# The first load of x: one transfer of 128 partitions, or two of 64 from two queues

## The chip, the cores and the metric

The kernel runs on one core of one Trainium2 chip. Times are device microseconds of one execution. The profile is that of one execution, taken by the hardware profiler; its times count from the first instruction of the program on the chip.

## The reference

`x` has shape 16 x 512 x 768 in float32, which is 8192 tokens of 768 numbers. `A` is 768 x 16 and `B` is 16 x 768. The result is x plus a low-rank correction of it:

```
def reference(x, A, B, scale):
    lora = np.matmul(np.matmul(x, A), B)
    return (x + scale * lora).astype(np.float32)
```

With scale 0.5. x is 25.2 MB and is read once, the result is 25.2 MB and is written once; A and B are small.

## The kernel before, in words

The 8192 tokens stand as 64 tiles of 128 partitions by 768 numbers. They are cut into five parts of 8, 8, 16, 16 and 16 tiles (`PARTS`). Within a part a partition holds consecutive tokens, so that a load of n tiles reads one stretch of n x 3 KB from memory for each partition. All of x lives in one SBUF tensor, `x_sb`, with room for 48 tiles; the last 16 tiles take the places of the first 16 once these are stored.

**Loads and stores.** All transfers are issued from SyncE's queue (SP), in a fixed order. There are eight loads of x (`LOADS`, L106): load 0 has the first 2 tiles (768 KB, 6 KB for each partition), load 1 the other 6 tiles of the first part (2304 KB), loads 2, 3 and 4 have 8 tiles each, load 5 has 16, and loads 6 and 7 have 8 each. The sum is written back into `x_sb`, and five stores (`STORES`) take whole parts out to memory. `on_sync` (L135) issues load 0, load 1, then three small transfers with A (L155) after a wait for a memset of `a_rows`, one with B (L159), then loads 2 to 5 (L160). Then it waits for sums and for TensorE's progress, issues stores 0 and 1 (L170), issues load 6 when store 0 has landed and load 7 when store 1 has, and issues the last three stores as their sums are ready. Each load has a semaphore of its own, which a transfer raises by 16 when it has landed.

**The work on a group.** The tiles are worked on in groups of eight. ScalarE (ACT) narrows the first four tiles of a group to float16 and GpSimd (POOL) the other four (`narrowed`, L186, L194). VectorE (DVE) transposes the group in 32 x 32 blocks (L250). TensorE (PE) multiplies by A, spread out in `w_bd` (L281), ScalarE scales the small product into `y_bd` (L238), TensorE multiplies by B (L302), and VectorE adds the result to x in place (L255), two tiles at a time.

**The first group** is narrowed in smaller pieces: GpSimd takes the two tiles of load 0 (L209), ScalarE the two after them and then the last four (L228, L229), all of load 1. GpSimd then waits for B (L211) and lays out the weights. `narrowed` waits for the semaphore of each load that its tiles come from, once for each engine and load (L188 to L191).

ScalarE's stream starts with `narrowed` for tiles 2 and 3; ahead of that the compiler puts the load of its function table.

Of the kernel before, what the change touches and what calls it, by code (L numbers as in the profile page):

```python
# [28 lines left out]
def kernel(  # L29
# [10 lines left out]
    P = 128  # L40
# [3 lines left out]
    x2 = x.flatten_outer_dims()  # L44
# [38 lines left out]
    def sem(name):  # L83
        sems.append(nc.alloc_semaphore(name))
        return sems[-1]
# [10 lines left out]
    def memory(t2, i, s, n):  # L96
        S = PARTS[i]
        return t2[ds(parts[i], S * P), :].rearrange("(p s) d -> p s d", s=S)[:, ds(s, n), :]

    def held(i, s, n):  # L100
        return tiles(where.index((i, s)), n)

    def tiles(t, n):
        return x_all[:, ds(t % ROOM, n), :]

    LOADS = [  # L106
        (0, 0, 2), (0, 2, 6), (1, 0, 8), (2, 0, 8), (2, 8, 8), (3, 0, 16), (4, 0, 8), (4, 8, 8)
    ]
    s_load = [sem(f"s_load{k}") for k in range(len(LOADS))]

    def load_of(t):
        i, s = where[t]
        return next(k for k, ld in enumerate(LOADS) if ld[0] == i and ld[1] <= s < ld[1] + ld[2])
# [18 lines left out]
    section = ExitStack()  # L132
    section.enter_context(tc.tile_critical(no_gpsimd_drain=True))  # L133

    def on_sync(e):  # L135
        def load(k):
            ld = LOADS[k]
            e.dma_start(out=held(*ld), in_=memory(x2, *ld)).then_inc(s_load[k], 16)  # L138

        def summed(k):  # L140
            e.wait_ge(s_sum, k + 1)
            if STORED[k] + 1 < NG:

                e.sem_inc(s_free[PAIRS - 1], 1)

        def store(k, done):
            st = STORES[k]
            e.dma_start(out=memory(out2, *st), in_=held(*st)).then_inc(done, 16)

        load(0)  # L150
        load(1)
        e.wait_ge(s_ready, 1)
        blocks = A.rearrange("(c e) r -> c (e r)", e=64)
        for c in range(SETS):
            e.dma_start(  # L155
                out=a_rows[c : SET * SET : SET, :], in_=blocks[ds(c * SET, SET), :]
            ).then_inc(s_a, 16)
        e.wait_ge(s_brows, 1)
        e.dma_start(out=b_rows[0 : R * APART : APART, :], in_=B).then_inc(s_b, 16)  # L159
        for k in range(2, len(LOADS) - 2):  # L160
            load(k)

        for p in range(2, PAIRS):
            e.sem_inc(s_free[p], 1)
        summed(0)
        summed(1)


        e.wait_ge(s_lora, 2 * PAIRS + 2)
        store(0, s_out0)  # L170
        store(1, s_out1)
        e.wait_ge(s_out0, 16)
        load(len(LOADS) - 2)
        e.wait_ge(s_out1, 16)
        load(len(LOADS) - 1)
        for k in range(2, len(STORES)):
            summed(k)
            if k == 2:


                e.wait_ge(s_raise, 6)
            store(k, s_out)
# [3 lines left out]
    def narrowed(e, copy, g, first, n=SUB):  # L186
        t = g * GROUP + first
        for k in dict.fromkeys(load_of(t + k) for k in range(n)):  # L188
            if (e, k) not in here:
                here.add((e, k))  # L190
                e.wait_ge(s_load[k], 16)  # L191
        if g:
            e.wait_ge(s_taken, g)
        ins = copy(out=xn[:, ds(first, n), :], in_=tiles(t, n))  # L194

        ins.then_inc(s_narrow if g else s_first if first else s_a, 1)

    def on_gpsimd(e):
        e.memset(a_rows[0:Q], 0.0).then_inc(s_ready, 1)  # L199
        e.memset(b_rows, 0.0).then_inc(s_brows, 1)  # L200
        e.memset(pick, 0.0).then_inc(s_pick, 1)
        e.memset(w_bd.rearrange("p c k m -> p (c k m)").bitcast(fp32), 0.0)  # L202
        e.memset(y_bd.rearrange("p s m -> p (s m)").bitcast(fp32), 0.0).then_inc(s_ready, 1)  # L203
        e.wait_ge(s_pick, 1)
        e.affine_select(  # L205
            out=pick, in_=pick, compare_op=mybir.AluOpType.not_equal, fill=1.0, base=0,
            pattern=[[0, NQ], [-APART, Q]], channel_multiplier=1,
        ).then_inc(s_pick, 1)
        narrowed(e, e.tensor_copy, 0, 0, SUB // 2)  # L209
        e.wait_ge(s_pick, 2)  # L210
        e.wait_ge(s_b, 16)  # L211
        e.tensor_copy(out=b_half, in_=b_rows).then_inc(s_bh, 1)  # L212
        e.wait_ge(s_ready, 3)
        e.tensor_copy(  # L214
            out=w_one.rearrange("i (c e) k r -> i c e (k r)", c=SETS),
            in_=a_t[0:Q].rearrange("i k r (e c) -> i c e (k r)", c=SET)[:, 0:SETS, 0:SET, :],
        ).then_inc(s_w, 1)
        e.wait_ge(s_w, 1)
        for b in range(NQ):
            e.tensor_copy(  # L220
                out=w_bd[ds(b * Q, Q), :, :, ds(b * Q, R)], in_=w_one
            ).then_inc(s_w, 1)
            e.wait_ge(s_w, b + 2)
        for g in range(1, NG):
            narrowed(e, e.tensor_copy, g, SUB)

    def on_scalar(e):
        narrowed(e, e.copy, 0, SUB // 2, SUB // 2)  # L228
        narrowed(e, e.copy, 0, SUB)  # L229
        e.wait_ge(s_bp, 1)  # L230
        e.copy(out=b_mm, in_=lora[0][:, 0, :]).then_inc(s_bm, 1)  # L231
        for g in range(NG):
            if g + 1 < NG:
                narrowed(e, e.copy, g + 1, 0)
            e.wait_ge(s_y, g + 1)
            for b in range(NQ):
                q = ds(b * Q, Q)
                last = e.mul(out=y_bd[q, :, q], in_=y_ps[q, :, :], mul=sc)  # L238
            last.then_inc(s_spread, 1)
# [33 lines left out]
    def on_tensor(e):  # L273
# [58 lines left out]
        for p in range(PAIRS):  # L332
            raised(p)

    on_sync(nc.sync)
    on_gpsimd(nc.gpsimd)
    on_scalar(nc.scalar)
    on_vector(nc.vector)
    on_tensor(nc.tensor)
# [44 lines left out]
```

## Time and profile before

| | |
|---|---|
| median of 3 runs | 123.55 us (123.45 to 123.71) |
| profiled execution, span | 121.9 us (the one time that the page gives of it) |
| bytes moved | 50.43 MB, 414 GB/s over the span |
| DMA packets' share of 16 engines' span | 96.8% |
| VectorE, the busiest compute engine | 81.7 us, 67% |
| load 0: issued from, to landing | 0.97 us, 4.5 us later |
| load 1: landing, as seen by ScalarE | 11.1 us |
| stores: last issued | 101.0 us, 20.0 us to landing |

The profile's groups are named by line, engine and operation; L138 is the line that issues loads of x, L148 the one that issues stores. A transfer's row on SP's queue (SPq) is the time in which the queue was issuing it; the transfer itself runs later, on 16 DMA engines. In the answers by window, the DMA column is the mean busy share of these 16 engines and the last column the rate of the bytes; a packet is counted in the window in which it starts, which is why a share can stand a little above 1.

### The profile page before, as it was taken

The numbers are of one execution on the slowest core, as the hardware profiler recorded it, in microseconds if no ns is written. First come the engines' busy times: TensorE is split into PE (matmuls) and PEld (weight loads), VectorE is DVE, ScalarE is ACT, GpSimd is POOL, SyncE is SP. The second block draws the span as 40 slices with busy tenths as digits, with TensorE's granted clock in tenths as the row PEclk, the third lists the DMA queues.
The fourth block names the chain that finished last, engine by engine and source line by source line (L and its number), as shares of the span: only waits on it lengthen the run. The fifth ranks groups of instructions, "written<-read, shape, count | busy, mean of one in ns | idle before, by whom it ended". The sixth has DMA issues, their size and how long they took to land.

```text
span 121.9 us, 885 instructions
## 1 busy us (share of the span) xinstructions
PE 50.5 (41%) x322; PEld 29.3 (24%) x322; DVE 81.7 (67%) x42; ACT 37.4 (31%) x43; POOL 28.4 (23%) x24
## 2 busy tenths in 40 slices
PE   0000239487457457647756714774674320000000
PEld 0000026244233233424424402442442110000000
DVE  0003850799999999999999959999995991000000
ACT  4003929444426402917230093643004000000000
POOL 7732638044026002607100090630000000000000
PEclk9999999999999999999999999999999985555555
DMA  3999999999997996999989999998998999899890
GB/s 67 421 429 429 443 443 403 451 435 419 476 516 339 435 516 298 460 403 443 443 363 460 427 427 468 451 484 387 419 500 387 403 516 403 371 516 419 355 516 0
DMA packets 1928, 50.43 MB, mean 414 GB/s; under 512 B 236, under 2 KB 236, under 8 KB 392
## 3 DMA queue, kind: packets, MB, share of 16 engines
q1 hardware_dynamic: 1928, 50.43, 96.8%
HBM read 25.26 MB, written 25.17 MB: 414 GB/s over the span
## 4 chain that ended last, share of the span: by engine, by line
DVE 33%; DMA 29%; PE 9%; ACT 6%; POOL 2%; issue 2%; SPq 0%; DVEq 0%
DVE x_sb L255 21%; DMA x_sb<-in_x_dram 20%; DVE xt L250 12%; DMA out_dram<-x_sb 9%; PE ps_yt L281 6%; ACT xn L194 3%; PE lora_ps L302 3%; ACT y_bd L238 2%; POOL xn L194 2%; SPq L138 0%; SPq L379 0%; DVEq L268 0%; SPq L133 0%
## 5 line engine op out<-in xcount | busy, mean ns | idle before, releaser
L255 DVE TENSOR_TENSOR x_sb<-x_sb,lora_ps 128x1536 f32<-128x1536 f32 x32 | 53.7, 1735 | 1.4 <-PE lora_ps L302 1.4
L302 PE MATMUL lora_ps<-b_mm,y_bd 128*128 128x512 f16 (+1 forms) x128 | 25.1, 328 | 23.7 <-ACT y_bd L238 15.3
L194 ACT CAST xn<-x_sb 128x3072 f16<-128x3072 f32 (+1 forms) x9 | 23.4, 2609 | 37.2 <-DMA x_sb<-in_x_dram 28.0
L250 DVE STREAM_TRANSPOSE xt<-xn 128x3072 f32<-128x3072 f32 (+1 forms) x9 | 27.0, 3005 | 6.7 <-PE ps_yt L281 4.9
L194 POOL CAST xn<-x_sb 128x3072 f16<-128x3072 f32 (+1 forms) x8 | 20.7, 2588 | 45.3 <-DMA x_sb<-in_x_dram 28.6
L281 PE MATMUL ps_yt<-xt,w_bd 128*128 128x256 f16 x192 | 25.7, 285 | 11.9 <-DVE xt L250 11.9
L281 PEld LDWEIGHTS ps_yt<-xt,w_bd 128*128 128x128 f16 x192 | 18.7, 100 | 19.6 <-issue 15.0
L302 PEld LDWEIGHTS lora_ps<-b_mm,y_bd 128*128 128x128 f16 x128 | 10.5, 97 | 36.8 <-ACT y_bd L238 17.5
L238 ACT ACTIVATE y_bd<-ps_yt 32x256 f16<-32x256 f32 x32 | 12.0, 374 | 17.7 <-PE ps_yt L281 17.4
L243 DVE STREAM_TRANSPOSE a_t<-a_rows 32x1024 f32<-32x1024 f32 x1 | 1.9, 1945 | 11.2 <-DMA a_rows<-in_A_dram 11.2
L315 PE MATMUL lora_ps<-b_half,pick 128*128 128x512 f16 (+1 forms) x2 | 0.8, 500 | 12.5 <-POOL b_half L212 12.5
L315 PEld LDWEIGHTS lora_ps<-b_half,pick 128*128 128x128 f16 x2 | 0.1, 105 | 12.5 <-issue 12.5
L220 POOL COPY w_bd<-w_one 32x384 f16<-32x384 f16 x4 | 2.0, 501 | 0.2
L212 POOL CAST b_half<-b_rows 128x768 f16<-128x768 f32 x1 | 0.8, 830 | 4.5 <-DMA b_rows<-in_B_dram 4.5
L194 ACT ACT_TABLE_LOAD x1 | 1.3, 1283 | 0.9 <-SPq L133 0.9
L202 POOL MEMSET w_bd<- 128x1536 f32 x1 | 1.4, 1372 | 0.0
L199 POOL MEMSET a_rows<- 32x1024 f32 x1 | 0.9, 941 | 0.5 <-SPq L133 0.5
L214 POOL CAST w_one<-a_t 32x384 f16<-32x384 f32 x1 | 0.8, 847 | 0.9 <-DVE a_t L243 0.9
L231 ACT CAST b_mm<-lora_ps 128x768 f16<-128x768 f32 x1 | 0.8, 798 | 0.0
L200 POOL MEMSET b_rows<- 128x768 f32 x1 | 0.7, 727 | 0.0
L203 POOL MEMSET y_bd<- 128x512 f32 x1 | 0.5, 514 | 0.0
L205 POOL TENSOR_SCALAR_AFFINE_SELECT pick<-pick 128x128 f16<-128x128 f16 x1 | 0.3, 300 | 0.0
(5 smaller groups left out, 0.6 us busy)
## 6 DMA issues: line engine op xcount, KB each, us to landing
out_dram<-x_sb SPq DMA_DIRECT2D x3, 6144.0 KB, 20.0
x_sb<-in_x_dram SPq DMA_DIRECT2D x5, 3072.0 KB, 14.8
x_sb<-in_x_dram SPq DMA_DIRECT2D x1, 6144.0 KB, 41.9
out_dram<-x_sb SPq DMA_DIRECT2D x2, 3072.0 KB, 14.9
x_sb<-in_x_dram SPq DMA_DIRECT2D x1, 2304.0 KB, 9.7
x_sb<-in_x_dram SPq DMA_DIRECT2D x1, 768.0 KB, 4.5
a_rows<-in_A_dram SPq DMA_DIRECT2D x3, 16.0 KB
b_rows<-in_B_dram SPq DMA_DIRECT2D x1, 48.0 KB, 7.4
```

The source lines that it names most:

```text
L194: ins = copy(out=xn[:, ds(first, n), :], in_=tiles(t, n))
L199: e.memset(a_rows[0:Q], 0.0).then_inc(s_ready, 1)
L202: e.memset(w_bd.rearrange("p c k m -> p (c k m)").bitcast(fp32), 0.0)
L212: e.tensor_copy(out=b_half, in_=b_rows).then_inc(s_bh, 1)
L220: e.tensor_copy(out=w_bd[ds(b * Q, Q), :, :, ds(b * Q, R)], in_=w_one).then_inc(s_w, 1)
L238: last = e.mul(out=y_bd[q, :, q], in_=y_ps[q, :, :], mul=sc)
L243: e.transpose(out=a_t[0:Q].rearrange("i k r c -> i (k r) c"), in_=a_rows[0:Q].rearrange("c (i k r) -> c (k r) i", k=2, r=R),).then_inc(s_r ...
L250: return e.transpose(out=ts[0], in_=ts[1])
L255: ins = e.tensor_tensor(out=xs, in0=xs, in1=lora[p % 2], op=mybir.AluOpType.add)
L281: mm = e.matmul(y_ps, w_bd[:, c, k, :], xv[:, :, c, :, k], start=(m == 0), stop=(m == MMS - 1),)
L302: mms.append(e.matmul(t[:, k, ds(n0, w)], y_bd[:, 2 * p + k, :], b_mm[:, ds(n0, w)], start=True, stop=True,))
L315: last = e.matmul(lora[0][:, 0, ds(n0, w)], pick.rearrange("p b r -> p (b r)"), b_half[:, ds(n0, w)], start=True, stop=True,)
```

## The change

Load 0 becomes two transfers of 64 partitions each, with the same bytes in the same places. SyncE's queue issues the lower half where it issued load 0 before, as its first transfer; ScalarE's queue issues the upper half as its first instruction, ahead of the function table's load and of its first narrowing. Both raise the same semaphore by 16, and the one wait that there is for load 0, GpSimd's ahead of its first narrowing, is for 32. All other transfers stay on SyncE's queue in the old order.

```
+    HALF = P // 2
+
+    def half_of_first(e, h):
+        ld, rows = LOADS[0], ds(h * HALF, HALF)
+        e.dma_start(out=held(*ld)[rows], in_=memory(x2, *ld)[rows]).then_inc(s_load[0], 16)
...
     def on_sync(e):
...
-        load(0)
+        half_of_first(e, 0)
         load(1)
         e.wait_ge(s_ready, 1)
...
             if (e, k) not in here:
                 here.add((e, k))
-                e.wait_ge(s_load[k], 16)
+                e.wait_ge(s_load[k], 16 if k else 32)
...
     def on_scalar(e):
+        half_of_first(e, 1)
         narrowed(e, e.copy, 0, SUB // 2, SUB // 2)
```

More of the change, by code (lines that the diff above doesn't have):

```diff
@@ L133, with half_of_first @@
     section.enter_context(tc.tile_critical(no_gpsimd_drain=True))
+    HALF = P // 2
+    def half_of_first(e, h):
+        ld, rows = LOADS[0], ds(h * HALF, HALF)
+        e.dma_start(out=held(*ld)[rows], in_=memory(x2, *ld)[rows]).then_inc(s_load[0], 16)
     def on_sync(e):
@@ L148, in store @@
             e.dma_start(out=memory(out2, *st), in_=held(*st)).then_inc(done, 16)
-        load(0)
+        half_of_first(e, 0)
         load(1)
@@ L190, in narrowed @@
                 here.add((e, k))
-                e.wait_ge(s_load[k], 16)
+                e.wait_ge(s_load[k], 16 if k else 32)
         if g:
@@ L227, in on_scalar @@
     def on_scalar(e):
+        half_of_first(e, 1)
         narrowed(e, e.copy, 0, SUB // 2, SUB // 2)
```

## The prediction

> **What bounds the kernel now.** I read the page's slices and queue lines first, to see which resource is never idle.
>
> ```profile
> span 121.9 us, 885 instructions
> PE 50.5 (41%) x322; PEld 29.3 (24%) x322; DVE 81.7 (67%) x42; ACT 37.4 (31%) x43; POOL 28.4 (23%) x24
> DMA  3999999999997996999989999998998999899890
> DMA packets 1928, 50.43 MB, mean 414 GB/s; under 512 B 236, under 2 KB 236, under 8 KB 392
> q1 hardware_dynamic: 1928, 50.43, 96.8%
> ```
>
> No compute engine is above 67%, and the DMA engines are busy 96.8% of the span; only the first slice and the last lack digits. Next come the windows, cut where the stream of bytes opens and closes.
>
> ```profile
> core 0: us, PE busy (x) PEld busy (x) DVE busy (x) ACT busy (x) POOL busy (x), PEclk, DMA share, GB/s
> 0.00:1.80 1.80, 0.00 (x0) 0.00 (x0) 0.00 (x0) 0.89 (x1) 1.05 (x5) 1.00 0.00 0
> 1.80:2.60 0.80, 0.00 (x0) 0.00 (x0) 0.00 (x0) 0.39 (x1) 0.80 (x3) 1.00 0.78 146
> 2.60:3.50 0.90, 0.00 (x0) 0.00 (x0) 0.00 (x0) 0.00 (x0) 0.90 (x2) 1.00 0.77 225
> 3.50:5.50 2.00, 0.00 (x0) 0.00 (x0) 0.00 (x0) 0.00 (x0) 1.30 (x3) 1.00 1.13 464
> 43.00:75.00 32.00, 18.00 (x122) 10.55 (x120) 30.69 (x16) 12.75 (x15) 8.25 (x3) 1.00 1.00 425
> 75.00:101.00 26.00, 14.46 (x94) 8.01 (x91) 24.63 (x14) 5.74 (x9) 2.75 (x1) 0.98 1.02 440
> 11.00:118.00 107.00, 50.50 (x322) 29.34 (x322) 81.73 (x42) 36.16 (x42) 22.92 (x13) 0.91 1.01 432
> 119.00:121.90 2.90, 0.00 (x0) 0.00 (x0) 0.00 (x0) 0.00 (x0) 0.00 (x0) 0.50 0.00 0
> ```
>
> Here the reader sees one stream. No byte moves before 1.8 us. From 1.8 to 3.5 the stream opens at 146 and then 225 GB/s. From there to 118 it runs with a share of 1.0 and 432 GB/s, and nowhere between 43 and 101, where loads and stores change places, does the share fall below 1. At 432 GB/s the 50.43 MB take 116.7 us. The opening adds its loss: 0.8 x 146 + 0.9 x 225 = 319 KB came in 1.7 us, which at 432 GB/s would have taken 0.74 us, so 0.96 us are lost. 1.8 + 0.96 + 116.7 = 119.5 us; the last store lands at 121.0 (below), and the 1.5 us between are the last packets' own time, unequal engines and the landing. The end of the span is therefore the start of the stream plus a fixed amount of bytes at a fixed rate. A change to load 0 can move it only by moving or reshaping the opening, unless it makes compute so late that the stream runs dry. So the slack of compute comes next.
>
> ```profile
> 0.91 1.28 ACT L194 ACT_TABLE_LOAD   x1 [0.91 <-SPq L133]
> 0.95 0.94 POOL L199 MEMSET a_rows<- 32x1024 f32 x1 [0.51 <-SPq L133]
> 0.97 0.85 SPq L138 DMA_DIRECT2D x_sb<-in_x_dram  x2
> 1.92 2.02 SPq L155 DMA_DIRECT2D a_rows<-in_A_dram  x3
> 4.57 2.03 SPq L138 DMA_DIRECT2D x_sb<-in_x_dram  x4
> 5.57 1.46 POOL L194 CAST xn<-x_sb 128x1536 f16<-128x1536 f32 x1 [0.73 <-DMA x_sb<-in_x_dram]
> 11.10 4.12 ACT L194 CAST xn<-x_sb 128x1536 f16<-128x1536 f32 x2 [8.91 <-DMA x_sb<-in_x_dram]
> 11.52 0.83 POOL L212 CAST b_half<-b_rows 128x768 f16<-128x768 f32 x1 [4.48 <-DMA b_rows<-in_B_dram]
> 43.92 0.82 SPq L148 DMA_DIRECT2D out_dram<-x_sb  x2
> 48.02 2.75 ACT L194 CAST xn<-x_sb 128x3072 f16<-128x3072 f32 x1 [5.66 <-DMA x_sb<-in_x_dram]
> 74.87 26.51 SPq L148 DMA_DIRECT2D out_dram<-x_sb  x3
> 77.40 2.75 ACT L194 CAST xn<-x_sb 128x3072 f16<-128x3072 f32 x1 [3.01 <-DMA x_sb<-in_x_dram]
> 101.04 0.33 SPq L148 DMA_DIRECT2D out_dram<-x_sb  x1
> ```
>
> ```profile
> out_dram<-x_sb SPq DMA_DIRECT2D x3, 6144.0 KB, 20.0
> L138 SPq DMA_DIRECT2D x_sb<-in_x_dram x1: 384/384/384, 1.0 to 1.0; - x1
> L138 SPq DMA_DIRECT2D x_sb<-in_x_dram x2: 384/396/407, 1.0 to 1.4; - x2
> L138 SPq DMA_DIRECT2D x_sb<-in_x_dram x8: 340/420/575, 1.0 to 62.7; - x8
> ```
>
> Each store is issued while earlier transfers still run. Stores 0 and 1 are issued at 43.92, and load 5 lands at 48.02, 4.1 us later. Store 2 is issued at 74.87, 2.5 us ahead of load 7's landing at 77.40. Its chain starts at load 6's landing, so it moves with the stream. The last store is issued at 101.04 and lands 20.0 us later (the median of the three large ones), of which 6.29 MB at 432 GB/s explain 14.6, so it stood in line for about 5 us. The chain of waits runs through VectorE and PE in these places, yet a chain later by a few tenths leaves the engines no idle time.
>
> **The change part by part.**
>
> *SyncE's issue.* Load 0's issue takes 384 ns now and becomes that of 64 partitions. The trace has no 64-partition issue. The bounds are zero saved and all of 384 ns saved. The eight loads take 340 to 575 ns, whether a partition's stretch is 6, 24 or 48 KB, so length of rows is no guide; I take nothing saved. If load 1 is issued up to 0.38 us earlier or, held up by the other queue, 0.41 us later (the longest of the first two issues), nothing follows: load 0's own packets keep the engines busy until load 0 lands at 0.97 + 4.5 = 5.5, and load 1's are in line from 1.82 on. Behind it SP waits for the memset of `a_rows`, which ends at 1.89, just before A's first issue at 1.92; a later load 1 would delay A, B and loads 2 to 5 by as much. Load 2 is issued at 4.57 and has its turn only after load 1, at about 11: 6 us of cover. Zero.
>
> *ScalarE's issue.* One more issue of 340 to 575 ns (I take 0.4) ahead of the function table's load, which is 1.28 from 0.91. ScalarE then stands idle for 8.91 us until load 1's landing at 11.10. It would be ready at 2.6 in place of 2.2. Zero; if the cover were gone it would be 0.4 us on the first cast.
>
> *The wait for 32.* GpSimd waits for both halves. Behind it stand its cast of 1.46 us and then the wait for B, 4.48 us long. The cast may start at 10.0 in place of 5.57 before B's cast, and VectorE's first transposes, feel it. Zero unless the upper half lands after 10.0. No other engine waits for load 0.
>
> *One more semaphore and 16 more packets of it.* Of the 1928 packets 236 are under 512 B and only raise semaphores; the other 1692 are one for each partition of a transfer (13 of 128, and 28 for A and B). One more small packet for each engine beside some 100 large ones: zero.
>
> *The opening itself.* This is the term that decides. In the window from 2.6 to 3.5 the engines are 77% busy at 225 GB/s, and later 101% at 432. So a byte takes (0.77/225) / (1.01/432) = 1.46 times the engine time: the packets of the opening are slow, beside the gaps. Load 0 is 786 KB; 319 KB have started by 3.5, and the other 467 KB go at the 464 GB/s of the next row. Two bounds:
> - Best, two queues feed each engine at once and fill the gaps and the slow reads: the 0.9 us at 225 GB/s run at 432. That gains 0.9 x (1 - 225/432) = 0.43 us.
> - Worst, halves of 64 partitions keep the opening's rate until load 0 is through: the 467 KB take 467/225 = 2.08 us in place of 1.01. That costs 1.07 us.
>
> Nothing in this trace shows a transfer of 64 partitions or a second queue. The row that it is nearest to is the opening's, since both halves are all of the opening and nothing else is in line ahead of them; and each engine, in place of eight packets of one transfer, gets four of each of two transfers that cover half the partitions. I take the middle of the two bounds, (1.07 - 0.43)/2 = 0.32 us, as a loss.
>
> [...]
>
> **Sum.** 0 + 0 + 0 + 0 + 0.32 us on the profiled span of 121.9, so about 122.2. The median of the runs shown is 123.55, 1.65 above that span; I take that as lying around the span and unchanged. 123.55 + 0.32 = 123.87 us.
>
> **The rivals.**
>
> *Nothing measurable* (within 0.2%, 0.25 us, which is about what a measurement of this kernel can tell): 123.55. For it: the same 1664 packets of loads and stores (13 x 128) pass the same engines, load 0's place in the stream stays, and every issue is covered. Against it: the opening's 1.7 us are the one uncovered stretch, and the change rewrites exactly these. [...]
>
> *Faster*: the mechanism is the best bound. The place is 1.8 to 3.5, the price 0.43 us, and it decides if ScalarE's packets reach the engines before about 2.6, while these are only 77% busy. For it: ScalarE is free at 0.91, 0.06 us ahead of SP's first issue. Against it: if the slow packets have their cause in memory, a second queue waits for the same. 123.55 - 0.43 = 123.1 us.
>
> *Half rate to the end of load 0*: the worst bound, 123.55 + 1.07 = 124.6. For it: both halves start together, and an engine's packets may meet the same neighbour at the same half again and again. Against it: two halves together cover all 128 partitions.
>
> *The halves do not run together*, because ScalarE's issue is late: load 1 stands in line behind the lower half, so the engines have work, and GpSimd has 4.4 us to spare. This gives 123.55 too and is counted with nothing.
>
> **How the numbers follow.** The forecast, a loss of 0.25 to 0.75 us, has 0.38. Half rate to the end has 0.08, nothing measurable 0.22, faster by more than 0.25 us 0.32. So slower has 0.46. I put the loss ahead of the gain because the bounds lie further out on that side. The forecast's own range is 123.8 to 124.3. The range for 8 in 10 must take in most of the faster case, down to 123.05, and the worst bound, 124.6.
>
> **What the profile of the changed kernel would show.** The opening's windows, 1.8 to 2.6 and 2.6 to 3.5, decide: below 146 and 225 GB/s, or a row from 3.5 to 5.5 below 464, and the forecast holds; 300 or more from 2.6 to 3.5 and the faster case does. ScalarE's first cast, 11.10 now, should be later by the term itself, about 11.4, and the last store's landing too. ScalarE's queue should show an issue of about 0.4 us near 0.9, its table load after it, and GpSimd's first cast should start well before 10. From 11 to 118 the rate should be 432 as now. I would be wrong altogether if that row changed, if a store were issued after the stream had run dry, or if the runs differed while the spans did not: then a second queue costs something around the span.

## The result, and the profile after

The changed kernel takes 125.28 us (median; 125.12 to 125.34) against 123.50 us (123.36 to 123.71) before: a ratio of 1.0145, 95% interval 1.0131 to 1.016, so 1.78 us slower. The forecast was 123.87 us with a range of 123.05 to 124.6. The direction was right, which was in part luck, as slower had a chance of 0.46; the time lies above the range.

The page of the changed kernel, its span, its queues and the landing times of the first transfers (line, engine, count, KB each, us from issue to landing):

```profile
span 123.5 us, 886 instructions
...
q1 hardware_dynamic: 1864, 50.04, 95.3%
q10 hardware_dynamic: 80, 0.39, 1.2%
...
x_sb<-in_x_dram SPq DMA_DIRECT2D x1, 2304.0 KB, 10.9
x_sb<-in_x_dram ACTq DMA_DIRECT2D x1, 384.0 KB, 4.3
x_sb<-in_x_dram SPq DMA_DIRECT2D x1, 384.0 KB, 6.0
```

The span grew by 1.6 us. The second queue (q10, ScalarE's) carries 64 packets of data and 16 that raise the semaphore. The two halves are issued 0.06 us apart, yet the upper half lands at 0.91 + 4.3 = 5.2 us and the lower one at 0.97 + 6.0 = 7.0. Before, the whole of load 0 landed at 5.5.

The halves run in turn. These are the queues' packets, MB and share, first of 1.8 to 3.6 us and then of 4.4 to 5.2:

```profile
q10 hardware_dynamic: 54, 0.33, 70.2%
```

```profile
q1 hardware_dynamic: 31, 0.19, 105.6%
```

Up to 3.6 only the upper half (q10) has packets, and from 4.4 on only SyncE's queue (q1), where the lower half stands first.

The same windows of the changed kernel as were shown of before (the last two numbers are the DMA share and GB/s):

```profile
core 0: us, PE busy (x) PEld busy (x) DVE busy (x) ACT busy (x) POOL busy (x), PEclk, DMA share, GB/s
0.00:1.80 1.80, 0.00 (x0) 0.00 (x0) 0.00 (x0) 0.29 (x1) 1.06 (x5) 1.00 0.00 0
1.80:2.60 0.80, 0.00 (x0) 0.00 (x0) 0.00 (x0) 0.80 (x1) 0.80 (x3) 1.00 0.57 123
2.60:3.50 0.90, 0.00 (x0) 0.00 (x0) 0.00 (x0) 0.19 (x1) 0.90 (x2) 1.00 0.83 239
3.50:5.50 2.00, 0.00 (x0) 0.00 (x0) 0.00 (x0) 0.00 (x0) 1.30 (x3) 1.00 1.24 289
5.50:11.00 5.50, 0.00 (x0) 0.00 (x0) 0.00 (x0) 0.00 (x0) 1.46 (x1) 1.00 0.95 380
...
11.00:118.00 107.00, 52.29 (x322) 30.36 (x322) 81.77 (x42) 36.20 (x42) 22.91 (x13) 0.90 1.01 436
```

Of before, for the windows that were not shown yet:

```profile
5.50:11.00 5.50, 0.00 (x0) 0.00 (x0) 0.00 (x0) 0.00 (x0) 1.46 (x1) 1.00 1.03 439
```

The opening itself, 1.8 to 3.5, moves 313 KB (0.8 x 123 + 0.9 x 239) in place of 319. The loss comes after it. From 3.5 to 5.5 the rate is 289 GB/s in place of 464, which is 350 KB less; from 5.5 to 11 it is 380 in place of 439, which is 325 KB less. Together with the opening's 6 KB that is 681 KB, or 1.58 us at 432 GB/s: the whole growth of the span. From 11 on the stream runs as before. All the while the engines are busy (shares of 1.24 and 0.95), so the packets are slow and not missing.

A finer cut of the second stretch, of the changed kernel:

```profile
6.00:8.00 2.00, 0.00 (x0) 0.00 (x0) 0.00 (x0) 0.00 (x0) 0.93 (x1) 1.00 0.73 304
8.00:11.00 3.00, 0.00 (x0) 0.00 (x0) 0.00 (x0) 0.00 (x0) 0.53 (x1) 1.00 1.02 436
```

and of before:

```profile
6.00:8.00 2.00, 0.00 (x0) 0.00 (x0) 0.00 (x0) 0.00 (x0) 1.03 (x1) 1.00 1.03 442
8.00:11.00 3.00, 0.00 (x0) 0.00 (x0) 0.00 (x0) 0.00 (x0) 0.00 (x0) 1.00 1.05 449
```

The slow stretch ends about when the lower half has landed, at 7.0. By then the engines are at load 1's packets already, and these are slow too. In order of time, of the changed kernel (start, duration, engine, and in brackets the idle time before and what ended it):

```profile
0.91 0.57 ACTq L139 DMA_DIRECT2D x_sb<-in_x_dram  x1
...
0.97 0.58 SPq L139 DMA_DIRECT2D x_sb<-in_x_dram  x1
1.51 1.28 ACT L200 ACT_TABLE_LOAD   x1 [1.51 <-SPq L133]
1.60 0.77 SPq L144 DMA_DIRECT2D x_sb<-in_x_dram  x1
...
7.07 1.46 POOL L200 CAST xn<-x_sb 128x1536 f16<-128x1536 f32 x1 [2.23 <-DMA x_sb<-in_x_dram]
12.52 4.12 ACT L200 CAST xn<-x_sb 128x1536 f16<-128x1536 f32 x2 [9.73 <-DMA x_sb<-in_x_dram]
...
13.11 0.83 POOL L218 CAST b_half<-b_rows 128x768 f16<-128x768 f32 x1 [4.58 <-DMA b_rows<-in_B_dram]
```

Each half takes 0.57 to 0.58 us to issue, longer than the 0.38 us of the whole load. GpSimd's cast starts 1.5 us later and still waits 4.58 us for B behind it, so that wait cost nothing. Load 1 reaches ScalarE at 12.52 in place of 11.10.

### The profile page after: what moved, and what is told of

The parts are those of the page before. It is cut to its first block, busy times and chain, and to the rows that moved or that the text cites. A ratio compares the mean times of both kernels' runs of the same rounds, so it can differ in the third digit from the quotient of the medians.

```text
span 123.5 us, 886 instructions
## 1 busy us (share of the span) xinstructions
PE 52.3 (42%) x322; PEld 30.4 (25%) x322; DVE 81.8 (66%) x42; ACT 37.5 (30%) x43; POOL 28.4 (23%) x24
## 4 chain that ended last, share of the span: by engine, by line
DVE 33%; DMA 29%; PE 10%; ACT 6%; POOL 2%; issue 2%; SPq 1%; DVEq 0%
DMA x_sb<-in_x_dram 21%; DVE x_sb L262 21%; DVE xt L257 12%; DMA out_dram<-x_sb 9%; PE ps_yt L288 6%; ACT xn L200 3%; PE lora_ps L309 3%; ACT y_bd L245 2%; POOL xn L200 2%; SPq L139 0%; SPq L386 0%; DVEq L275 0%; SPq L133 0%
## 5 line engine op out<-in xcount | busy, mean ns | idle before, releaser
L309 PE MATMUL lora_ps<-b_mm,y_bd 128*128 128x512 f16 (+1 forms) x128 | 26.3, 341 | 22.0 <-ACT y_bd L245 14.5
L288 PE MATMUL ps_yt<-xt,w_bd 128*128 128x256 f16 x192 | 26.7, 292 | 11.4 <-DVE xt L257 11.4
L288 PEld LDWEIGHTS ps_yt<-xt,w_bd 128*128 128x128 f16 x192 | 19.3, 103 | 19.5 <-issue 14.5
L309 PEld LDWEIGHTS lora_ps<-b_mm,y_bd 128*128 128x128 f16 x128 | 11.0, 100 | 35.4 <-ACT y_bd L245 16.9
```

The lines of the kernel that those rows point to most:

```text
L288: mm = e.matmul(y_ps, w_bd[:, c, k, :], xv[:, :, c, :, k], start=(m == 0), stop=(m == MMS - 1),)
L309: mms.append(e.matmul(t[:, k, ds(n0, w)], y_bd[:, 2 * p + k, :], b_mm[:, ds(n0, w)], start=True, stop=True,))
```

## The experiments

Three theories stood at first. P: a transfer of the lower or the upper 64 partitions runs at about half the rate, from whichever queue. Q: using a second queue is what costs. O: halves cost only in the opening. Where no ratio is given below, the time is that of one execution; 19 executions of the kernel before beside the first four of these runs lie between 123.34 and 123.93 us.

**Both halves from one queue.**

```
-        half_of_first(e, 0)
+        half_of_first(e, 0)
+        half_of_first(e, 1)
         load(1)
...
     def on_scalar(e):
-        half_of_first(e, 1)
```

> Both 64-partition halves of load 0 are issued from SyncE's queue, one behind the other; ScalarE issues nothing. Theory P (a transfer of partitions 0 to 63, or 64 to 127, runs at about half the rate, whichever queue issues it): slower than before by 1 to 2 us, 124.5 to 125.5, and the windows of load 0 stay near 215 to 290 GB/s until about 6 us. Theory Q (the cost is that a second queue is used at all): no change, 123.3 to 123.8.

Measured: 125.52 us against 123.63, ratio 1.0164 (1.0132 to 1.0196). Three of its windows:

```profile
2.60:3.50 0.90, 0.00 (x0) 0.00 (x0) 0.00 (x0) 0.00 (x0) 0.90 (x2) 1.00 0.62 225
3.50:5.50 2.00, 0.00 (x0) 0.00 (x0) 0.00 (x0) 0.00 (x0) 1.30 (x3) 1.00 1.13 255
5.50:11.00 5.50, 0.00 (x0) 0.00 (x0) 0.00 (x0) 0.00 (x0) 1.46 (x1) 1.00 0.97 379
```

The loss is there without ScalarE's queue, with the same two slow windows (255 and 379 GB/s, beside 289 and 380 of the changed kernel). Q falls as the cause.

**Two queues, but cut by tiles**: each transfer has one tile and all 128 partitions.

```
     def half_of_first(e, h):
-        ld, rows = LOADS[0], ds(h * HALF, HALF)
-        e.dma_start(out=held(*ld)[rows], in_=memory(x2, *ld)[rows]).then_inc(s_load[0], 16)
+        ld = (0, h, 1)
+        e.dma_start(out=held(*ld), in_=memory(x2, *ld)).then_inc(s_load[0], 16)
```

> Load 0 is two transfers from the two queues as in the change, but cut by tiles: each has one tile and all 128 partitions. Theory P: no loss from the rate, 123.3 to 123.9, with 464 GB/s or so again from 3.5 to 5.5 us. Theory Q: as the changed kernel, 124.9 to 125.4.

Measured: 123.74 us against 123.63, ratio 1.0013 (1.0003 to 1.0022).

```profile
1.80:2.60 0.80, 0.00 (x0) 0.00 (x0) 0.00 (x0) 0.80 (x1) 0.80 (x3) 1.00 0.81 115
2.60:3.50 0.90, 0.00 (x0) 0.00 (x0) 0.00 (x0) 0.03 (x1) 0.90 (x2) 1.00 0.86 266
3.50:5.50 2.00, 0.00 (x0) 0.00 (x0) 0.00 (x0) 0.00 (x0) 1.30 (x3) 1.00 1.19 449
```

Two queues and two transfers cost at most 0.3 us. They do not open the stream faster either: 331 KB by 3.5 in place of 319, but then 449 GB/s in place of 464.

**Load 0 whole from ScalarE's queue**, load 1 first on SyncE's.

```
     def on_sync(e):
-        load(0)
         load(1)
...
     def on_scalar(e):
+        ld = LOADS[0]
+        e.dma_start(out=held(*ld), in_=memory(x2, *ld)).then_inc(s_load[0], 16)
```

> Load 0 whole, 128 partitions, from ScalarE's queue; load 1 becomes SyncE's first transfer. Theory P: 123.3 to 123.9; the two issues meet, so the first bytes may come up to 0.3 us later. Theory Q: slower, 124.3 to 125.4, since a second queue is used and the engines must serve both.

Measured: 123.74 us against 123.63, ratio 1.002 (0.9994 to 1.0046). No difference is shown, and there is no gain from the earlier issue. Load 0 runs beside load 1 here: it lands 10.4 us after its issue, and GpSimd's first cast starts at 11.41. Even so late a cast costs nothing in the end.

**Halves in the middle of the stream**: load 0 as before, load 3 (3.15 MB) as two transfers on SyncE's queue.

```
+            if k != 3:
...
+            for h in range(2):
+                rows = ds(h * (P // 2), P // 2)
+                e.dma_start(out=held(*ld)[rows], in_=memory(x2, *ld)[rows]).then_inc(s_load[k], 16)
...
-                e.wait_ge(s_load[k], 16)
+                e.wait_ge(s_load[k], 16 * 2 if k == 3 else 16)
```

> Load 0 as before; load 3 (8 tiles, 3.15 MB, in the middle of the stream, about 18 to 25 us) is two transfers of 64 partitions, both from SyncE's queue. Theory P: its 7.3 us become 14.6, so the time is about 130.8 us, and some 7 us of the windows after 18 us show about 216 GB/s. Theory Q: no change, 123.5. A theory O that halves cost only in the opening, where packets are slow anyway: no change, 123.5.

Measured: 132.15 us, 8.5 above the kernel before (123.63).

```profile
18.00:33.00 15.00, 10.77 (x63) 6.50 (x61) 10.01 (x5) 4.25 (x5) 2.74 (x1) 1.00 1.00 208
```

and of the kernel before:

```profile
18.00:33.00 15.00, 10.39 (x65) 6.47 (x64) 11.01 (x6) 8.50 (x10) 5.49 (x2) 1.00 1.06 455
```

For 15 us the DMA engines are busy all the time (share 1.00) at 208 GB/s. Here nothing opens and no second queue is used, so O falls, and P has its rate: 208/432 = 0.48. The loss is above the forecast of 7.3 by 1.2 us.

The next question was what about a half makes it slow: the number of its partitions (theory N) or which ones they are (theory S, by sides: all below 64, all from 64 on, or some of both). By S a quarter is as slow as a half.

**Quarters**: load 3 as four transfers of 32 partitions in order, the loop and the wait above with 4 in place of 2.

> Load 3 as four transfers of 32 partitions (0 to 31, 32 to 63 and so on), all from SyncE's queue. [...] Theory N (the rate falls with the number of partitions): a quarter of the rate, about 145 us and 105 GB/s.

Measured: 132.27 us.

```profile
18.00:33.00 15.00, 11.84 (x64) 7.14 (x61) 9.52 (x5) 4.16 (x5) 2.74 (x1) 0.89 1.00 206
```

A quarter is as slow as a half and no slower.

**Even and odd partitions** of load 3, still two transfers of 64 from SyncE's queue:

```
-                rows = ds(h * (P // 2), P // 2)
+                rows = slice(h, P, 2)
```

> Load 3 as two transfers of 64 partitions, the even ones and the odd ones, both from SyncE's queue. Theory S: each half has partitions on both sides, so the rate is between 300 and 432 GB/s and the time 123.5 to 127 us. Theory N: half the rate as with lower and upper halves, about 132 us.

Measured: 123.57 us against 123.58.

```profile
18.00:33.00 15.00, 10.51 (x62) 6.30 (x60) 10.40 (x6) 8.44 (x10) 5.49 (x2) 1.00 1.06 455
```

All of the 8.5 us are gone with 64 partitions in each transfer. N falls, S stands: blocks of 64 or 32 partitions that lie all below or all above 64 ran at 208 and 206 GB/s, and 64 partitions from both sides at the full 455. A block across 64, such as 32 to 95, was not run, so that the border is at 64, and that the spacing of the partitions plays no part, is not shown.

One more rival is not tested by itself. A partition always reads the same place in memory, so a cut by sides also reads from a shorter stretch of memory at a time. Against it: load 1 of the kernel before reads from a stretch (128 x 24 KB) as long as that of a half of load 3 (64 x 48 KB), and its window from 5.5 to 11 has 439 GB/s; and quarters, with half of that stretch, are no slower than halves.

**The change itself, cut by even and odd** (`slice(h, P, 2)` for `rows` in `half_of_first`):

> The change with another cut: the two transfers of load 0, from SyncE's and ScalarE's queues, have the even and the odd partitions in place of the lower and the upper 64. Theory S: most of the loss is gone, 123.5 to 124.4; what stays is the longer issue of a 64-partition transfer, 0.2 to 0.3 us. Theory N: as the changed kernel, 124.9 to 125.4.

Measured: 124.11 us against 123.58, ratio 1.0043 (1.0028 to 1.0059), which is 0.53 us.

```profile
1.80:2.60 0.80, 0.00 (x0) 0.00 (x0) 0.00 (x0) 0.80 (x1) 0.80 (x3) 1.00 0.57 77
2.60:3.50 0.90, 0.00 (x0) 0.00 (x0) 0.00 (x0) 0.18 (x1) 0.90 (x2) 1.00 0.66 150
3.50:5.50 2.00, 0.00 (x0) 0.00 (x0) 0.00 (x0) 0.00 (x0) 1.29 (x3) 1.00 1.08 442
```

In order of time, its two issues:

```profile
0.91 0.56 ACTq L139 DMA_DIRECT2D x_sb<-in_x_dram  x1
...
0.97 0.58 SPq L139 DMA_DIRECT2D x_sb<-in_x_dram  x1
```

The slow stretch after 3.5 is gone; what stays is a slower opening, 197 KB by 3.5 in place of 319, or 0.28 us at 432 GB/s. It comes with the longer issue; that it comes from it is not shown. The other 0.25 us of the 0.53 are not placed.

**One load in place of loads 0 and 1**, a try for a faster kernel.

```
-        (0, 0, 2), (0, 2, 6), (1, 0, 8), ...
+        (0, 0, 8), (1, 0, 8), ...
...
         load(0)
-        load(1)
```

> A try for a faster kernel: loads 0 and 1 are one transfer of 8 tiles and 128 partitions from SyncE's queue (24 KB for each partition). The opening's slow packets are 64 to 128 fewer. If the slowness is by packet, up to 0.3 us faster, 123.2; if it is by engine or by byte, no change, 123.4 to 123.8. GpSimd's first cast starts at about 11 instead of 5.6, and the stream hides that.

Measured: 123.79 us against 123.58, ratio 1.0023 (0.9999 to 1.0047). No gain.

The last question was why two halves from two queues did not share the two sides between them. In the changed kernel the lower half landed 1.8 us after the upper one, and their packets ran in turn. Would they share if both stood ready on every engine at once? The two runs that follow were taken on another chip.

**Control: load 1 in halves from one queue**, load 0 as before.

```
         load(0)
-        load(1)
+        half_of_second(e, 0)
+        half_of_second(e, 1)
```

`half_of_second` is `half_of_first` with load 1, and the wait for load 1 is for 32.

> Control: load 0 whole as before; load 1 (2.36 MB) as lower and upper 64 partitions, both from SyncE's queue, one behind the other. At 208 GB/s in place of 432 it takes 11.3 us in place of 5.5: about 129.4 us.

Measured: 129.07 us, beside 123.97 of one execution of the kernel before.

**Load 1's halves side by side**: `tile_of_first` is the cut by tiles of above.

```
         # SyncE
+        tile_of_first(e, 0)
+        half_of_second(e, 0)
...
         # ScalarE
+        tile_of_first(e, 1)
+        half_of_second(e, 1)
```

> Load 0 by tiles from the two queues (one tile each, 128 partitions), and behind these load 1's lower 64 partitions from SyncE's queue and its upper 64 from ScalarE's, so that both halves stand ready on every engine at the same time. Theory T (halves side by side use both sides, the loss is only that they run one after the other): 123.5 to 125.5. Theory L (engines stay in step and meet on one side at a time): about 129, as the control.

Measured: 129.11 us. Two of its windows, and the landing times of the two halves:

```profile
7.50:9.50 2.00, 0.00 (x0) 0.00 (x0) 0.00 (x0) 0.00 (x0) 0.15 (x1) 1.00 0.85 203
9.50:11.50 2.00, 0.00 (x0) 0.00 (x0) 0.00 (x0) 0.00 (x0) 0.00 (x0) 1.00 1.08 258
```

```profile
x_sb<-in_x_dram ACTq DMA_DIRECT2D x1, 1152.0 KB, 13.8
x_sb<-in_x_dram SPq DMA_DIRECT2D x1, 1152.0 KB, 15.0
```

The halves, issued 0.06 us apart, land 1.3 us apart after some 14 us, so they were in flight together, and the loss is that of the control, 5.1 us. Halves do not make each other good. The packets of the queues show why. From 5.3 to 12.9 us, in six windows one behind the other (to 6.7, 8.1, 9.3, 10.5, 11.7 and 12.9):

```profile
q10 hardware_dynamic: 16, 0.29, 100.7%
q1 hardware_dynamic: 16, 0.29, 90.2%
q10 hardware_dynamic: 16, 0.29, 102.7%
q1 hardware_dynamic: 16, 0.29, 103.0%
q10 hardware_dynamic: 16, 0.29, 103.5%
q1 hardware_dynamic: 16, 0.29, 103.5%
```

In each window 16 packets start, as many as there are DMA engines, and all are of one half; in the next window all are of the other. The view doesn't name the engines; shares of 0.90 to 1.04 fit one packet for each. So the engines alternate between the halves in step, which is theory L.

## Why the prediction was wrong in size

*What bounds the kernel* held. The stream from 11 to 118 runs at 436 GB/s, compute stays covered, and the span grew by what the stream lost before 11 us.

*SyncE's issue* was taken as nothing saved, between 0 and 384 ns saved. That bracket was wrong on its other side: a 64-partition issue takes 0.58 us in place of 0.38, with or without the other queue, and load 1's issue behind it takes 0.77 us and ends at 2.37, 0.55 us later than before where 0.41 was allowed. The run with the even and odd halves has both with full rate after it, and is 0.53 us slower, of which 0.28 stand in the opening's windows. Nothing in the opening covers the first issue, so the bound should have reached to a loss.

*ScalarE's issue* (0.57 us ahead of its table load), *GpSimd's wait for 32* (cast at 7.07, 4.58 us still to wait) and *the 16 packets* (the cut by tiles has them too, at a ratio of 1.0013) cost nothing that a run shows, as said.

*The opening itself* is the step that failed, by its size: 0.32 us were taken, the middle between a gain of 0.43 and a loss of 1.07, and the whole came to 1.78. Two things were wrong in it. The gain was no real end: a second queue opened nothing faster in the cut by tiles (1.0013). And the loss was reckoned from 3.5 us on with the 467 KB not yet started, at 225 GB/s, as if load 1 behind it ran at full rate. The window from 6 to 8 shows load 1 slow as well (304 in place of 442), until the lower half has landed. Of the 1.58 us found in the windows, 0.81 lie between 3.5 and 5.5; the 0.75 behind that stand in no bound. The 225 GB/s of the worst bound was the rate of a 128-partition load in the opening; that it lies near the rate of a half, 208, was luck. With the rate of a half known, the sum would have been near: 1/208 - 1/432 is 2.49 us for each MB. The estimates and what was measured:

| cut into halves | MB | at 2.49 us per MB | measured |
|---|---|---|---|
| load 0 (the change) | 0.786 | 1.96 | 1.78 |
| load 1, one queue | 2.36 | 5.9 | 5.1 |
| load 3, one queue | 3.15 | 7.8 | 8.5 |

The rate comes from load 3 itself, so its row is no test. For load 0 the agreement is in part luck too: with the 0.53 us of the even and odd cut on top, the sum would be 2.5, so the two losses don't simply add.

*The rivals.* Nothing measurable is refuted by the result (1.0131 to 1.016). What was said for it, the same packets through the same engines, left the rate out: the halves ran in turn, from 4.4 to 5.2 us the lower one alone with 0.19 MB in 0.8 us, some 238 GB/s. The faster case is refuted by the cut by tiles and by load 0 from ScalarE. The case of half rate to the end of load 0 was right in kind (halves ran at 208 GB/s in place of 432 in the middle of the stream), with a chance of 0.08 and too small a price. What was said for it, a neighbour met again and again, is the author's conjecture; no view names the engines. What was put against it, that two halves together cover all 128 partitions, is refuted by load 1's halves side by side (129.11 us beside 129.07). The halves that do not run together, counted with nothing, came true in the order of the packets, though it was SyncE's half that waited for ScalarE's. Its price of zero was wrong: the engines had work, as it says, but at half the rate.

*The signs.* The row from 3.5 to 5.5 fell below 464 (289), by which the forecast was to hold; it named no size, so it could not tell a loss of 0.32 from one of 1.78. ScalarE's first cast, at 12.52 in place of about 11.4, could.

## What to carry to other kernels

A load from memory into SBUF, in a stream that is bound by DMA, should not be cut into blocks of partitions that lie all below or all above 64. Here lower and upper halves of loads of 0.8 to 3.1 MB cost 1.8 to 8.5 us, on one queue or two, side by side or in turn; in the middle of the stream they ran at 208 GB/s in place of 432. Stores were not tried. If such a load must be cut, cut it along the free dimension, here by tiles (a ratio of 1.0013 to the uncut load), or in the middle of the stream by even and odd partitions (123.57 beside 123.58). When a change halves the partitions of a transfer and no row of the trace has such a transfer, all its bytes at half the stream's rate are the estimate to take, though it is no ceiling: here 0.786 MB at 216 GB/s in place of 432 would take 1.82 us more, beside 1.78 measured, and load 3's 3.15 MB would take 7.3, beside 8.5. What stands behind it in the queue was delayed as well: load 1 reached ScalarE at 12.52 us in place of 11.10.

## What was not expected of the hardware

As the first transfer of a queue, one of 64 partitions took longer to issue than one of 128: 0.56 to 0.58 us against 0.38 to 0.40, with either cut and with one queue or two. Behind other transfers the two overlapped: 0.34 to 0.58 us for the loads of the kernel before, 0.59 to 0.77 for the whole load 1 behind a half, 0.52 to 0.61 for load 3's halves and 0.42 to 0.44 for its quarters. With first transfers of 64 partitions the stream opened later. The first 0.3 us of the stream, of the changed kernel:

```profile
1.80:2.10 0.30, 0.00 (x0) 0.00 (x0) 0.00 (x0) 0.30 (x1) 0.30 (x2) 1.00 0.00 0
```

and of the kernel before:

```profile
1.80:2.10 0.30, 0.00 (x0) 0.00 (x0) 0.00 (x0) 0.30 (x1) 0.30 (x2) 1.00 0.64 102
```

No packet starts before 2.1 in the changed kernel, nor in the two others whose first transfers have 64 partitions; with the cut by tiles 72 GB/s move in that window. The cause of the longer issue stays open. Two transfers issued 0.06 us apart from two queues landed 1.8 us apart when each had 64 partitions, and 0.66 us apart (4.2 and 4.8 us after issues at 0.91 and 0.97) when each had 128; why the first are taken in turn is not settled. The rows of the cut by tiles for the last, and its queues from 1.8 to 3.5 us, where both have packets:

```profile
x_sb<-in_x_dram ACTq DMA_DIRECT2D x1, 384.0 KB, 4.2
x_sb<-in_x_dram SPq DMA_DIRECT2D x1, 384.0 KB, 4.8
```

```profile
q10 hardware_dynamic: 67, 0.21, 57.2%
q1 hardware_dynamic: 41, 0.13, 26.2%
```
